# The overflow branch moved into the ninth expert pair, the meta tokens' reads put last, the 16 by 16 inversion cut into two 8 by 8 halves, and the first transfers reordered

## The chip, the core and the metric

The kernel runs on one core of a Trainium2 chip. The metric is device microseconds of one execution; the lower, the better. The core has TensorE (PE; its weight loads are listed as PEld), VectorE (DVE), ScalarE (ACT), GpSimd (POOL) and SyncE (SP, which here only issues DMAs); 16 DMA engines serve all queues.

## What is computed

Two layers over 528 tokens (16 meta tokens ahead of 512), 1024 channels. Cut to what matters here:

```python
for l in range(2):
    proj = h @ w_in[l]
    o_dn = deltanet_group(...)    # 4 heads; chunks need inv(I + L), L strictly lower
    o_sa = dsa_group(...)         # 8 heads, each query keeps its best 128 keys
    mix = concat(o_dn, o_sa) @ w_out[l]
    h = layer_norm(alpha * h + mix, ln1_g[l], ln1_b[l])
    ffn = hier_moe(h, ...)        # top group of 4, top 2 of its 8 experts, 32 experts
    h = layer_norm(alpha * h + ffn, ln2_g[l], ln2_b[l])
return h[:, 16:]                  # hid = silu(t @ w1) * (t @ w3); y = hid @ w2, gated
```

## The kernel before, in words

One program, both layers unrolled. A framework tracks which instruction reads and writes which tile and sets all waits. A planner, working with its own cost estimates, decides the order of each engine's queue; the order of the source is its priority, and `tc.issue_after(x)` asks that instructions of x's engine stand behind x. Each engine then runs its queue strictly in order. Large tiles (128 x 2112, fp32) come from one pool of 19 `unit`s: two hold the residual `hu`, the expert weights take most of the others.

**Start.** `begin` (L229) issues on SP six transfers: router weights `gw`, `lcol`, and four small ones (`ng`, and `alog`, `dtb`, `br` broadcast to all partitions by `bcast`, L153). Behind them come the first projection's weights `wr` (`weights`, L216: a load, for this block a scaling on POOL, L240, a rounding on ACT, L221, a remainder on POOL, L226), tiles 3 and 4 of x, the constants, the rotary tables.

**Attention part.** The list ORDER names projections, index scores, key selections, and for each pair of heads H, P (prepare), I (invert), R, E. `invert` (L647) gathers the 66 diagonal 16 by 16 blocks of I + L onto 66 partitions by a DMA round trip (`scr`), and DVE substitutes forward, row by row: 15 steps of one product (L668, up to 15 by 15 per partition) and one sum (L670). A second round trip (`scx`, L673, L675) puts the inverses back; PE then joins blocks of 16 to 32, 64 and 128 (tiles `y`, `d`), interleaved with projections. There are two inversions in each layer.

**After attention.** `w_out`, the first layer norm's statistics, routing (L1149 to L1237, a chain of some 40 short DVE instructions) and, beside it, the normalisation of the five row tiles: tiles 2 and 4 on POOL (L1111), the others on ACT (L1113); each is stored to `hs`, from which the experts' rows are gathered.

**Experts.** 32 experts in 16 pairs, 64 slots each. A pair needs six 1 MB weight loads (`load_part`, L311, tile `we`, one unit each), a gather of its rows (POOL, L1242), their transposes (`xtq`, L1372; `xT`, L1377 and L1379), 32 matmuls (`h`), the activation, 16 matmuls (`yp`), and a scatter of the gated rows into the table `ytab` (POOL, L1491); pairs 14 and 15 stay in SBUF (`yw`). Before the first pair 16 loads have been issued. In pair 2 a unit `lnu` is taken for the first norm's gain and bias; in pair 4 PE spreads them over the partitions (`lnp`), in pairs 5 and 6 DVE applies them to the residual (`rescale`, L1419). In layer 0, pair 8 also issues `begin` for the next layer.

**Overflow.** An expert with more than 64 tokens has its rest worked off under `tc.If(n_extra > 0)` (L1505), behind the last pair: a loop that loads that expert again, adds into the residual, and uses four units. With these inputs `n_extra` is 0 and the branch is jumped over in both layers; every engine still runs it.

**The layer's end.** In pair 15 `fetch_rows` (L1429; meta tile L1434) reads the two contributions of each row back from `ytab` in the order of the norm list, in layer 0 tiles 1, 2, meta, 3, 4, in layer 1 tiles 1 to 4; then the second norm's rows (`row_quarters`, L168; `lnw`, L1468). DVE adds them to the residual (`merge_rows`, L1440). Behind the branch PE adds pairs 14 and 15 (`cmb`), DVE adds that to the residual (L1407), and the second norm follows (L1618 to L1646); then the next layer's first projection, or the output.

Of the kernel before, what the change touches and what calls it, by code (L numbers as in the profile page):

```python
# [16 lines left out]
F32 = mybir.dt.float32  # L17
# [47 lines left out]
def trunk(ctx, tc, a, out, dbg=None, depth=DEPTH, stop=None):  # L65
# [163 lines left out]
    def begin(l):  # L229
# [4 lines left out]
        nc.sync.dma_start(lcol, a["ln1_c"][l])  # L234
        ng = spool.tile([P, 1], F32, name="ng")
        nc.sync.dma_start(ng, a["ng"][l])
        return gw, lcol, ng, bcast(a["alog"], l, 4, "alog"), bcast(a["dtb"], l, 4, "dtb"), bcast(a["b_r"], l, 36, "br")
# [36 lines left out]
    for l in range(depth):  # L274
# [372 lines left out]
        def invert(Hs, LT, full):  # L647


            Db, Xb, tm = Hs[0].spare[:, 0:256], Hs[0].spare[:, 256:512], Hs[1].spare[:, 0:256]  # L650
# [12 lines left out]
            Dv = Db.rearrange("p (j i) -> p i j", j=16)  # L663
            Xr = Xb.rearrange("p (r c) -> p r c", r=16)
            Xv = Xb.rearrange("p (r c) -> p c r", r=16)
            tv = tm.rearrange("p (r c) -> p r c", r=16)
            for i in range(1, 16):
                nc.vector.tensor_tensor(tv[:NB, :i, :i], Xv[:NB, :i, :i], Dv[:NB, i:i + 1, :i].to_broadcast([NB, i, i]),  # L668
                                        op=OP.mult)
                nc.vector.tensor_reduce(Xr[:NB, i, :i], tv[:NB, :i, :i], axis=AX.X, op=OP.add, negate=True)  # L670
            X16 = tm[:, :128].rearrange("p (q c) -> p q c", q=8)
# [641 lines left out]
        def expert_hidden(xT, ws):  # L1313

            cs = range(len(ws[0]))
            n = 64 * len(cs)
            p1 = pa("h13")
            for k in range(KT):
                for c in cs:
                    fed = _mm(nc, p1[64 * c:64 * c + 64], xT[:, k, 64 * c:64 * c + 64],  # L1320
                              ws[k // 2][c][:, k % 2 * 512:k % 2 * 512 + 512], start=(k == 0), stop=(k == KT - 1))
# [6 lines left out]
        def expert_out(hid, ws):  # L1328

            cs = range(len(ws[0]))  # L1330
            n = 64 * len(cs)
# [6 lines left out]
            for j in range(2):  # L1338
                for f in range(2):
                    for c in cs:  # L1340
                        fed = _mm(nc, p3[j][64 * c:64 * c + 64], hidT[:, f * n + 64 * c:f * n + 64 * c + 64],
                                  ws[j][c][:, 512 * f:512 * f + 512], start=(f == 0), stop=(f == 1))
            return p3, fed

        def gated(p3, gate, yh, yl, n=P):

            for j in range(2):
                p = p3[j][:n]
                done = nc.scalar.activation(yh[j][:n], p, AF.Copy, scale=gate[:n])
                nc.vector.scalar_tensor_tensor(yl[j][:n], p, gate[:n], yh[j][:n], op0=OP.mult, op1=OP.subtract)  # L1350
# [7 lines left out]
        def slots(toks, tag="r"):  # L1358

            G = tpool.tile([P, T + 3], F32R, name="G", tag=tag, bufs={"t": 5, "r": 2}[tag])  # L1360
# [3 lines left out]
        def halves(name, tag):  # L1364
            return [tpool.tile([P, T + 3], F32R, name=name, tag=tag, bufs=5)[:, 0:512] for j in range(2)]
# [44 lines left out]

        rowed, merged, late = {}, {}, []
# [10 lines left out]
        def fetch_rows():  # L1422

            for t in norder:
                o = OFF[t] - q0
                if t:
                    merged[t] = unit(f"yr{t}")
                    for i in range(2):
                        nc.sync.dma_start(merged[t][:, i * D:(i + 1) * D], ytab[i * rows + o:i * rows + o + P, :])  # L1429
                else:  # L1430
                    merged[t] = lnwq[:, 6 * D // 4:2 * D]
                    for i in range(2):
                        for q in range(4):
                            nc.sync.dma_start(merged[t][32 * q:32 * q + 16, i * D // 4:(i + 1) * D // 4],  # L1434
                                                ytab[i * rows:i * rows + 16, q * D // 4:(q + 1) * D // 4])
# [6 lines left out]
        for pair in range(16):  # L1442
            if pair == 8 and l + 1 < depth:
                with tc.issue_after(loaded[0].ins):
                    begun = begin(l + 1)
            if pair == 2:
# [11 lines left out]
            if pair == 15:  # L1458
# [4 lines left out]
                fetch_rows()  # L1463
                if 0 in tiles_q:
                    row_quarters(lnwq, 1, l)
                for i, nm in enumerate(("_g", "_b")):
                    src = a["ln2" + nm]
                    nc.sync.dma_start(lnw[:, i * D:(i + 1) * D],  # L1468
                                      bass.AP(tensor=src.tensor, offset=src.offset + l * D, ap=[[0, P], [1, D]]))
# [4 lines left out]
            hid, fed = expert_hidden(xT, ws[:4])  # L1474
            if pair == 0:
                gate_table()
            if pair == 4:
# [9 lines left out]
            p3, fed = expert_out(hid, ws[4:])  # L1487
# [14 lines left out]
        ttab = dpool.tile([1024 + P, 1], I32, name=f"ttab{l}")  # L1502
        wtab = dpool.tile([1024 + P, 1], F32, name=f"wtab{l}")
        etab = dpool.tile([16, 64], I32, name=f"etab{l}")
        with tc.If(n_extra > 0):  # L1505
            ov = unit("ov")
            area[:] = [ov[:, 0:T], 0]
            none = spool.tile([P, 9], I32, name="none", bufs=1)
            nc.vector.memset(none, 4096)
            nc.sync.dma_start(ttab[:, :].rearrange("(p c) o -> p (c o)", p=P), none)  # L1510
            zero = spool.tile([P, 9], F32, name="zero", bufs=1)
            nc.vector.memset(zero, 0.0)
            nc.sync.dma_start(wtab[:, :].rearrange("(p c) o -> p (c o)", p=P), zero)

            cum = [ov[:, (i + 1) * T:(i + 2) * T] for i in range(2)]
            nc.vector.tensor_copy(cum[0][:, :32], nb)
            ci = 0
            for s in (1, 2, 4, 8, 16):
                nc.vector.tensor_copy(cum[1 - ci][:, :s], cum[ci][:, :s])
# [230 lines left out]
```

## Time and profile before

| | us |
|---|---|
| median of 3 runs | 1441.79 (1438.68 to 1449.44) |
| the profiled execution's own time | 1439.81 |
| its span, first to last instruction | 1438.0 |
| around the span | 1.8 |

The mean granted TensorE clock of the profiled execution is 0.944 of full speed. The span falls into these stretches: layer 0's attention part to about 380, `w_out` and routing to 455, its experts to 699, its end to 732; in layer 1 the same at 1085, 1157, 1405 and 1438. A timeline row reads: start, length, engine, source line, operation, tiles written and read, how many in a row, and in brackets the idle time ahead of the first and what ended it. A letter q behind an engine marks its queue (waits, branches and DMA issues).

### The profile page before, as it was taken

The numbers are of one execution on the slowest core, as the hardware profiler recorded it, in microseconds if no ns is written. First come the engines' busy times: TensorE is split into PE (matmuls) and PEld (weight loads), VectorE is DVE, ScalarE is ACT, GpSimd is POOL, SyncE is SP. The second block draws the span as 40 slices with busy tenths as digits, with TensorE's granted clock in tenths as the row PEclk, the third lists the DMA queues.
The fourth block names the chain that finished last, engine by engine and source line by source line (L and its number), as shares of the span: only waits on it lengthen the run. The fifth ranks groups of instructions, "written<-read, shape, count | busy, mean of one in ns | idle before, by whom it ended". The sixth has DMA issues, their size and how long they took to land.

```text
span 1438.0 us, 23990 instructions
## 1 busy us (share of the span) xinstructions
PE 1262.4 (88%) x8664; PEld 896.7 (62%) x8664; DVE 794.0 (55%) x2088; ACT 542.3 (38%) x1385; POOL 596.5 (41%) x779
## 2 busy tenths in 40 slices
PE   6999999899996997888578999998999699978884
PEld 6998998787893332222268988997887443322222
DVE  4887999767336131111578889996663531311126
ACT  3574544355322222222136655352552122222222
POOL 4557497845023112111154584897332232111102
PEclk9999999899997999999899999998799899998997
DMA  4252222223716999999721531322255389999982
GB/s 168 82 194 76 68 83 86 71 90 128 282 61 257 392 409 372 410 410 397 288 96 68 198 89 58 101 83 67 75 212 228 140 329 409 409 409 410 409 334 81
DMA packets 103692, 306.55 MB, mean 213 GB/s; under 512 B 24567, under 2 KB 25671, under 8 KB 103568
## 3 DMA queue, kind: packets, MB, share of 16 engines
q1 hardware_dynamic: 88464, 274.11, 50.4%
q0 software_dynamic: 9184, 18.00, 3.4%
q10 hardware_dynamic: 5920, 12.85, 2.4%
q8 instruction: 70, 1.15, 0.3%
q14 instruction: 54, 0.44, 0.1%
HBM read 281.49 MB, written 32.19 MB: 218 GB/s over the span
## 4 chain that ended last, share of the span: by engine, by line
PE 25%; DVE 12%; issue 6%; ACT 3%; DMA 2%; POOL 2%; SPq 1%; POOLq 0%; DVEq 0%; ACTq 0%; another core or an unknown queue 0%
PE h L61 7%; PE pj L61 5%; PE yp L61 4%; DVE scores L496 2%; DVE top L495 2%; PE po L986 1%; DMA ytab<-yw,dest 1%; DVE dn L668 1%; PE lgp L61 1%; PE d L61 1%; DVE dn L521 1%; PE xtq L1372 1%; PE ptp L978 1%; PE y L61 1%; POOL wl L226 1%
## 5 line engine op out<-in xcount | busy, mean ns | idle before, releaser
L226 POOL TENSOR_TENSOR wl<-wr,wh 128x256 fp32r<-128x256 f32 (+1 forms) x296 | 251.9, 881 | 218.2 <-ACT wh L221 177.9
L61 PE MATMUL h<-we,xT 128*64 128x512 f32 x1024 | 229.3, 599 | 0.2
L61 PE MATMUL pj<-hh,wh 128*128 128x264 f32 (+2 forms) x928 | 163.2, 312 | 5.5 <-ACT raw L338 1.9
L61 PEld LDWEIGHTS h<-we,xT 128*64 128x64 f32 x1024 | 73.6, 140 | 145.2 <-issue 133.4
L61 PE MATMUL yp<-we,hidT 128*64 128x512 f32 x512 | 139.5, 684 | 26.8 <-ACT yw L1354 23.1
L61 PE MATMUL pj<-hl,wh 128*128 128x264 f32 (+2 forms) x928 | 161.0, 307 | 0.9 <-DVE rs L1623 0.9
L61 PE MATMUL pj<-hh,wl 128*128 128x264 f32 (+2 forms) x928 | 160.7, 306 | 0.2 <-POOL wl L226 0.2
L61 PEld LDWEIGHTS pj<-hh,wh 128*128 128x128 f32 (+1 forms) x928 | 133.7, 195 | 12.3 <-ACT raw L338 2.1
L1241 POOL MEMSET xe<- 128x1024 f32 x32 | 30.4, 952 | 267.3 <-PE h L61 252.4
L61 PEld LDWEIGHTS pj<-hl,wh 128*128 128x128 f32 (+1 forms) x928 | 135.1, 193 | 7.0 <-DVE rs L1623 1.1
L61 PEld LDWEIGHTS pj<-hh,wl 128*128 128x128 f32 (+1 forms) x928 | 132.0, 191 | 5.5 <-issue 0.4
L1324 DVE SCALAR_TENSOR_TENSOR hid<-hid,h 128x256 f32<-128x256 f32 x32 | 13.5, 421 | 214.1 <-ACT hid L1323 214.1
L221 ACT CAST wh<-wr 128x1024 fp32r<-128x1024 f32 (+1 forms) x82 | 85.5, 1045 | 88.0 <-PE pj L61 38.5
L1323 ACT ACTIVATE hid<-h 128x256 f32<-128x256 f32 x32 | 12.3, 383 | 229.3 <-PE h L61 217.8
L1379 ACT ACTIVATE xT<-xtq,lcol 128x128 f32<-128x128 f32 x192 | 73.4, 455 | 59.3 <-PE xtq L1372 58.7
L61 PEld LDWEIGHTS yp<-we,hidT 128*64 128x64 f32 x512 | 35.8, 149 | 95.3 <-issue 58.4
L1377 DVE TENSOR_SCALAR xT<-xtq,lcol 128x128 f32<-128x128 f32 x64 | 26.2, 410 | 119.9 <-ACT xT L1379 119.9
L521 DVE SCALAR_TENSOR_TENSOR dn<-cin,cw,dn 128x528 f32<-128x528 f32 x72 | 64.0, 898 | 10.0 <-ACT dn L519 8.9
L1491 POOL DMA_INDIRECT ytab<-yw,dest x28 | 28.2, 1005 | 88.7 <-ACT xT L1379 45.8
L496 DVE MATCH_REPLACE8 scores<-top,scores 128x144 f32<-128x144 f32 (+3 forms) x128 | 62.0, 487 | 0.1
L495 DVE MAX8 top<-scores 128x8 f32<-128x144 f32 (+3 forms) x128 | 60.5, 494 | 0.3
L1334 PE MATMUL hidT<-cst,hid 128*128 128x128 f32 x64 | 14.0, 300 | 39.7 <-DVE hid L1325 39.7
(432 smaller groups left out, 2434.9 us busy)
## 6 DMA issues: line engine op xcount, KB each, us to landing
we<-w SPq DMA_DIRECT2D x190, 1024.0 KB, 19.1
wr<-w_in SPq DMA_DIRECT2D x64, 512.0 KB, 3.3
wr<-w_out SPq DMA_DIRECT2D x16, 512.0 KB, 3.7
yr<-ytab SPq DMA_DIRECT2D x16, 512.0 KB, 10.5
ytab<-zr ACTq DMA_DIRECT2D x16, 264.0 KB, 3.3
hu<-x SPq DMA_DIRECT2D x8, 512.0 KB, 5.3
hs<-hu ACTq DMA_DIRECT2D x8, 512.0 KB, 4.8
ytab<-zr ACTq DMA_DIRECT2D x16, 256.0 KB, 3.2
```

What stands on the lines that cost most here:

```text
L61: return nc.tensor.matmul(out, lhsT=lhsT, rhs=rhs, start=start, stop=stop)
L221: nc.scalar.copy(hi[:, :KT * m], raw)
L226: eng.tensor_tensor(lo[:, c], raw[:, c], hi[:, c], op=OP.subtract)
L495: nc.vector.max(top, sc)
L496: nc.vector.match_replace(out=sc, in_to_replace=top, in_values=sc, imm_value=GONE)
L521: nc.vector.scalar_tensor_tensor(dst, cin[:, j:j + T], cw[:, ci + j:ci + j + 1], dst, op0=OP.mult, op1=OP.add)
L668: nc.vector.tensor_tensor(tv[:NB, :i, :i], Xv[:NB, :i, :i], Dv[:NB, i:i + 1, :i].to_broadcast([NB, i, i]), op=OP.mult)
L978: nc.tensor.transpose(p[:, (tk - 1) * P:tk * P], lg[:, OFF[tk]:OFF[tk] + P], ident)
L1241: nc.gpsimd.memset(xe, 0.0)
L1377: last = nc.vector.tensor_scalar(xT[:, kk, :], src, g_, b_, op0=OP.mult, op1=OP.add)
L1379: nc.scalar.activation(xT[:, kk, :], src, AF.Identity, bias=b_, scale=g_)
L1491: nc.gpsimd.indirect_dma_start(out=ytab[:, :], out_offset=bass.IndirectOffsetOnAxis(ap=dest[:, pair:pair + 1], axis=0), in_=yw[:, :], in_o ...
```

## The change

1. The overflow branch becomes a function, called at the top of pair 8 in each layer, behind the loads of pairs 8, 9 and 10. Its body loads its weights into other tiles, takes no unit, and writes its rows through `ytab`; after pair 15 there is no branch. `lnu` is taken in pair 6 in place of 2, `lnp` moves from pair 4 to 9, `rescale` from pairs 5 and 6 to 10 and 11.
2. `fetch_rows` takes one tile: tiles 1 to 4 are read first, then the second norm's rows, `row_quarters`, and the meta tile last. The four large tiles' merges stand together in pair 15; the meta tile's moves into its own `norm_stats`. The next layer's first weights are asked for behind the last of the norm's rows on SP.
3. The inversion treats both diagonal 8 by 8 blocks of each 16 by 16 block in the same instructions (7 steps) and gets the lower left block by two products of 512 elements and two sums.
4. `begin` is split: at the start, the four small transfers go behind the first weights, tiles 3 and 4 of x, and the constants.
5. All five tiles are normalised on ACT.

The diff, cut to its core:

```diff
-    begun = begin(0)
-    begun += (weights(0, 32, MISC, extra=begun[:2]),)
+    begun = begin_router(0)
+    first = weights(0, 32, MISC, extra=begun)
     fetch(h, spill, (3, 4))
     nc.sync.dma_start(cst[:, P:], a["cst"][:, P:])
+    begun += (*begin_rest(0), first)
     tables = rotary()
...
-            for i in range(1, 16):
-                nc.vector.tensor_tensor(tv[:NB, :i, :i], Xv[:NB, :i, :i], Dv[:NB, i:i + 1, :i].to_broadcast([NB, i, i]), op=OP.mult)
-                nc.vector.tensor_reduce(Xr[:NB, i, :i], tv[:NB, :i, :i], axis=AX.X, op=OP.add, negate=True)
+            for i in range(1, 8):
+                tv = tm[:NB, :2 * i * i].rearrange("p (b c r) -> p b c r", b=2, c=i)
+                nc.vector.tensor_tensor(tv, Xd[:, :, :i, :i].rearrange("p b r c -> p b c r"),
+                                        Dd[:, :, None, :i, i].to_broadcast([NB, 2, i, i]), op=OP.mult)
+                nc.vector.tensor_reduce(Xd[:, :, i, :i], tv, axis=AX.X, op=OP.add, negate=True)
+            for a_, b_, dst, neg in (...):
+                nc.vector.tensor_tensor(prod, a_[:, :, None, :].to_broadcast([NB, 8, 8, 8]),
+                                        b_[:, None, :, :].to_broadcast([NB, 8, 8, 8]), op=OP.mult)
+                nc.vector.tensor_reduce(dst, prod, axis=AX.X, op=OP.add, negate=neg)
...
-            if t in (2, 4):
-                nc.gpsimd.tensor_scalar(x, x, rs[:n, t:t + 1], nmr[:n, t:t + 1], op0=OP.mult, op1=OP.add)
-            else:
-                nc.scalar.activation(x, x, AF.Identity, bias=nmr[:n, t:t + 1], scale=rs[:n, t:t + 1])
+            nc.scalar.activation(x, x, AF.Identity, bias=nmr[:n, t:t + 1], scale=rs[:n, t:t + 1])
...
         for pair in range(16):
+            if pair == 8:
+                for ahead in range(3):
+                    load_pair(8 + ahead)
+                overflow()
             if pair == 8 and l + 1 < depth:
                 with tc.issue_after(loaded[0].ins):
-                    begun = begin(l + 1)
-            if pair == 2:
+                    begun = begin_router(l + 1) + begin_rest(l + 1)
+            if pair == 6:
                 lnu = unit("lnu")
...
-                fetch_rows()
+                for t in norder:
+                    if t:
+                        fetch_rows(t)
+                for i, nm in enumerate(("_g", "_b")):
+                    last_read = nc.sync.dma_start(lnw[:, i * D:(i + 1) * D], ...)
                 if 0 in tiles_q:
                     row_quarters(lnwq, 1, l)
-                for i, nm in enumerate(("_g", "_b")): ...
-                with tc.issue_after(fed.ins):
-                    for t in norder[:2]:
-                        merge_rows(t)
+                    fetch_rows(0)
...
-            if pair == 4:
+            if pair == 9:
                 with tc.issue_after(fed.ins):
                     for r in rowed["gb"]:
                         row_bcast(r)
-            if pair in (5, 6):
-                rescale(torder[:3] if pair == 5 else torder[3:])
+            if pair in (10, 11):
+                rescale(torder[:3] if pair == 10 else torder[3:])
             if pair == 15:
                 with tc.issue_after(fed.ins):
-                    for t in norder[2:]:
-                        merge_rows(t)
+                    for t in norder:
+                        if t:
+                            merge_rows(t)
...
-            with tc.issue_after(done.ins):
+            with tc.issue_after(done.ins), tc.issue_after(last_read.ins):
                 begun += (weights(l + 1, 32, MISC, extra=begun[:2]),)
-        with tc.If(n_extra > 0):
-            ov = unit("ov")
...
         def norm_stats(t, evac, mode):
+            if t == 0:
+                merge_rows(t)
```

## Rows read from the trace of the kernel before

**Rows 1.** Page, part 1: busy us (share of the span), instructions.

```profile
PE 1262.4 (88%) x8664; PEld 896.7 (62%) x8664; DVE 794.0 (55%) x2088; ACT 542.3 (38%) x1385; POOL 596.5 (41%) x779
```

**Rows 2.** Windows, layer 1's experts: PE, PEld, DVE, ACT, POOL; clock, DMA share, GB/s.

```profile
1170.00:1270.00 100.00, 90.33 (x407) 31.25 (x402) 24.54 (x41) 25.75 (x62) 19.85 (x20) 0.97 1.02 407
1270.00:1380.00 110.00, 89.64 (x384) 30.87 (x382) 16.27 (x34) 25.43 (x62) 16.86 (x18) 0.91 1.02 408
```

**Rows 3.** DMA issues from 1170 to 1380: count, KB each, median us to landing.

```profile
we<-w SPq DMA_DIRECT2D x75, 1024.0 KB, 20.7
ytab<-yw,dest POOLq DMA_INDIRECT x13, 8.0
```

**Rows 4.** Chain of waits, layer 1: start, us, `h` of pairs 3, 4, 5, 8, 9.

```profile
1198.61 7.04 PE h L61 x32
...
1212.22 7.04 PE h L61 x32
...
1232.08 6.89 PE h L61 x32
...
1276.85 7.58 PE h L61 x32
...
1294.19 7.44 PE h L61 x32
```

**Rows 5.** Timeline, layer 0's end.

```profile
684.04 1.76 SPq L1429 DMA_DIRECT2D yr<-ytab  x4
...
687.21 13.22 SPq L1434 DMA_DIRECT2D lnwq<-ytab  x8
...
711.95 7.16 PE L61 MATMUL cmb<-yw,G 128*128 128x512 f32 x48 [12.50 <-DVEq L1505]
...
714.03 0.69 DVE L1407 CUSTOM_DVE_ANT_0 hu<-hu,cmb 128x512 f32<-128x512 f32 x1 [2.29 <-PE cmb L61]
```

**Rows 6.** Source line L1440, both layers: ns min/median/max, first and last start.

```profile
L1440 DVE TENSOR_TENSOR hu<-hu,yr x16: 1211/1218/1695, 698.9 to 1411.6; 128x1024 f32<-128x1024 f32 x16
```

**Rows 7.** Timeline, layer 1's end.

```profile
1389.44 4.76 SPq L1429 DMA_DIRECT2D yr<-ytab  x8
...
1413.03 3.75 PE L61 MATMUL cmb<-yw,G 128*128 128x512 f32 x8 [7.83 <-DVEq L1505]
...
1415.11 0.69 DVE L1407 CUSTOM_DVE_ANT_0 hu<-hu,cmb 128x512 f32<-128x512 f32 x1 [2.29 <-PE cmb L61]
```

**Rows 8.** Waits, whole span: us in total, times, longest.

```profile
PE y L61 <- DVE scores L681: 13.7, 4, 5.3
```

**Rows 9.** Windows, behind layer 1's second inversion; columns as Rows 2.

```profile
1000.00:1010.00 10.00, 10.00 (x161) 8.89 (x156) 2.29 (x6) 3.96 (x9) 0.00 (x0) 0.50 0.07 24
```

**Rows 10.** Timeline, the start.

```profile
3.54 0.63 SPq L236 DMA_DIRECT2D ng<-ng  x1
...
5.82 0.33 SPq L216 DMA_DIRECT2D wr<-w_in  x1
...
12.52 0.67 POOL L240 TENSOR_TENSOR wr<-gw,lcol 128x288 f32<-128x288 f32 x1 [11.08 <-DMA wr<-w_in]
```

**Rows 11.** Groups by line, the substitution: busy us, mean ns of one.

```profile
L668 DVE TENSOR_TENSOR dn<-dn 66x1 f32<-66x1 f32 (+14 forms) x60 | 30.6, 509 | 2.9 <-DMA dn<-scr 1.5
...
L670 DVE TENSOR_REDUCE dn<-dn 66x1 f32<-66x1 f32 (+14 forms) x60 | 13.9, 232 | 1.4
```

**Rows 12.** Source line L579: ns min/median/max.

```profile
L579 DVE TENSOR_TENSOR dk<-ktp,Bc x8: 676/678/680, 82.3 to 960.6; 128x512 f32<-128x512 f32 x8
```

**Rows 13.** Timeline, layer 0's routing.

```profile
437.02 0.35 DVE L1151 TENSOR_TENSOR rta<-rta 128x180 f32<-128x180 f32 x1
...
438.54 1.22 DVE L1153 TENSOR_TENSOR rta<-rta,br 128x180 f32<-128x180 f32 x1
```

**Rows 14.** Source line L1505, layer 1: SP's branch and its nine waits.

```profile
L1505 SPq EVENT_SEMAPHORE  x9: 17/17/17, 1395.8 to 1405.6; - x9
...
L1505 SPq COMPARE_BRANCH  x1: 50/50/50, 1395.3 to 1395.3; - x1
```

More of the change, by code (lines that the diff above doesn't have):

```diff
@@ L227, in weights, with begin_router @@
         return hi, lo
-    def begin(l):
+    def begin_router(l):
         gw = spool.tile([P, KT, 36], F32, name="gw", bufs=1)
@@ L234, in begin, with begin_rest @@
         nc.sync.dma_start(lcol, a["ln1_c"][l])
+        return gw, lcol
+    def begin_rest(l):
         ng = spool.tile([P, 1], F32, name="ng")
         nc.sync.dma_start(ng, a["ng"][l])
-        return gw, lcol, ng, bcast(a["alog"], l, 4, "alog"), bcast(a["dtb"], l, 4, "dtb"), bcast(a["b_r"], l, 36, "br")
+        return ng, bcast(a["alog"], l, 4, "alog"), bcast(a["dtb"], l, 4, "dtb"), bcast(a["b_r"], l, 36, "br")
     def scaled_router(dst, gw, lcol):
@@ L662, in invert @@
             nc.gpsimd.memset(Xb[:, 0:256:17], 1.0)
[L663 to L666, printed above, removed]
[L667 to L671 removed]
+            Dd, Xd = (H.spare[:NB, 0:272].rearrange("p (b x) -> p b x", b=2)[:, :, 0:128].rearrange("p b (r c) -> p b r c", r=8)
+                      for H in Hs)
+            for i in range(1, 8):
[3 more added lines that the diff above has]
+                nc.vector.tensor_reduce(Xd[:, :, i, :i], tv, axis=AX.X, op=OP.add, negate=True)
+            half = Hs[0].spare[:NB, 400:464].rearrange("p (j c) -> p j c", j=8)
+            prod = tm[:NB].rearrange("p (a c k) -> p a c k", a=8, c=8)
+            Xr = Xb[:NB].rearrange("p (r c) -> p r c", r=16)
+            Lr = Db[:NB].rearrange("p (j i) -> p i j", j=16)
+            for a_, b_, dst, neg in ((Lr[:, 8:, :8], Xr[:, :8, :8].rearrange("p k c -> p c k"), half, False),
+                                     (Xr[:, 8:, 8:], half.rearrange("p k c -> p c k"), Xr[:, 8:, :8], True)):
+                nc.vector.tensor_tensor(prod, a_[:, :, None, :].to_broadcast([NB, 8, 8, 8]),
+                                        b_[:, None, :, :].to_broadcast([NB, 8, 8, 8]), op=OP.mult)
+                nc.vector.tensor_reduce(dst, prod, axis=AX.X, op=OP.add, negate=neg)
+            X16 = Hs[0].spare[:, 272:400].rearrange("p (q c) -> p q c", q=8)
             scx = dpool.tile([NB, 256], F32, name="scx", bufs=2)
@@ L1313, in expert_hidden @@
         def expert_hidden(xT, ws):
-            cs = range(len(ws[0]))
-            n = 64 * len(cs)
             p1 = pa("h13")
             for k in range(KT):
+                if k % 2 == 0:
+                    w = ws(k // 2)
+                cs = range(len(w))
+                n = 64 * len(cs)
                 for c in cs:
                     fed = _mm(nc, p1[64 * c:64 * c + 64], xT[:, k, 64 * c:64 * c + 64],
-                              ws[k // 2][c][:, k % 2 * 512:k % 2 * 512 + 512], start=(k == 0), stop=(k == KT - 1))
+                              w[c][:, k % 2 * 512:k % 2 * 512 + 512], start=(k == 0), stop=(k == KT - 1))
             hid = mpool.tile([P, 2 * P], F32, name="hid", tag="vnew")[:n]
@@ L1328, in expert_out @@
         def expert_out(hid, ws):
-            cs = range(len(ws[0]))
-            n = 64 * len(cs)
+            n = hid.shape[0]
+            cs = range(n // 64)
             p2 = pb("hidT")
@@ L1356, in gated_rows, with slots @@
             return done
-        def slots(toks, tag="r"):
-            G = tpool.tile([P, T + 3], F32R, name="G", tag=tag, bufs={"t": 5, "r": 2}[tag])
+        def slots(toks):
+            G = tpool.tile([P, T + 3], F32R, name="G", tag="r", bufs=2)
             nc.gpsimd.tensor_scalar(G[:, 0:T - q0], tid[:, 0:T - q0], toks, None, op0=OP.is_equal)
             return G
-        def halves(name, tag):
-            return [tpool.tile([P, T + 3], F32R, name=name, tag=tag, bufs=5)[:, 0:512] for j in range(2)]
         def transpose_rows(xe, xT):
@@ L1420, in rescale, with fetch_rows @@
                 nc.vector.scalar_tensor_tensor(x, b_, ALPHA, x, op0=OP.mult, op1=OP.add)
[L1422 to L1435, printed above, removed]
+        def fetch_rows(t):
+            o = OFF[t] - q0
+            if t:
+                merged[t] = unit(f"yr{t}")
+                for i in range(2):
+                    nc.sync.dma_start(merged[t][:, i * D:(i + 1) * D], ytab[i * rows + o:i * rows + o + P, :])
+            else:
+                merged[t] = lnwq[:, 6 * D // 4:2 * D]
+                for i in range(2):
+                    for q in range(4):
+                        nc.sync.dma_start(merged[t][32 * q:32 * q + 16, i * D // 4:(i + 1) * D // 4],
+                                          ytab[i * rows:i * rows + 16, q * D // 4:(q + 1) * D // 4])
         def merge_rows(t):
```

188 lines of the change are left out of this document (96 added, 92 removed).

## The prediction, made before the changed kernel ran

> **What bounds the kernel now.** I read the page's busy times first, then windows by stage, then the chain of waits, the waits by pair of engines, and timelines of each layer's end and of the start. TensorE is busy 1262.4 us of 1438.0 [rows 1], so 176 us of idle time are the most that better order alone could give, and most of that lies where transfers set the pace.
>
> In the experts the DMA engines do. From 1170 to 1380 their share reads 1.02 at 407 and 408 GB/s in both windows, while PE has 90% [rows 2]; 75 loads went out in these 210 us, 2.8 us for each with all that shares the engines [rows 3]. The chain shows both paces: 13.6 us from pair 3's `h` to pair 4's, when weights asked for earlier lie ready (PE's own pace), 17.3 from pair 8's to pair 9's, when six loads have to arrive (6 x 2.8 = 16.8) [rows 4]. Pair 4 takes 19.9: it holds `lnp`, which adds 6.2.
>
> At the layer ends DVE and its branch do. In layer 0, `yr` of the first two tiles is issued at 684.04, SP then issues the meta tile's eight reads for 13.22 us, so tiles 3 and 4 follow only at about 700.5; PE, free at 711.95 - 12.50 = 699.45, waits for the branch in DVE's queue [rows 5], which stands behind the merges (1.22 us each) [rows 6]. In layer 1 PE is free at 1413.03 - 7.83 = 1405.2 and waits for the same; the merges' last begins at 1411.6 [rows 6, 7].
>
> In the attention part PE is almost never idle, but at each of the four inversions it waits for the chain through DVE, 13.7 us in all, the longest 5.3 [rows 8]. Behind such a wait it can run on at half clock: 0.50 over 1000 to 1010, with PE busy all 10 us [rows 9].
>
> **The change part by part.** *Start, -2 us.* Four small transfers stand ahead of the first weights, from 3.54 to 5.82, and POOL waits 11.08 us for these until 12.52 [rows 10]. Moved behind, they give up to 2.3. The large transfers for x now share the engines with nothing new ahead of `wr`; the small ones are needed by router and gates much later. Range 0 (x's tiles set the start as well) to 3 gained; I take 2.
>
> *Inversions, -7.* Now 15 products (mean 509 ns) and 15 sums (232 ns) take 11.1 us of DVE each time [rows 11]. Afterwards 7 small products and 7 sums remain; with two blocks at once they have up to 98 elements per partition, inside the sizes of today's, so below the mean: I take 330 and 190 ns, 3.6 us. The two products of 512 elements are priced by a product of that size, 0.68 each [rows 12], the sums over the same 512 as much: 2.7 together. So 6.4 in place of 11.1: 4.7 less in each of the four chains. The waits that can shrink are 2.9, 4.1, 1.4 and 5.3 us (the total and the longest are in [rows 8]): at most 2.9 + 4.1 + 1.4 + 4.7 = 13.1. Against taking all: DVE is nearly full there, and what a shorter chain frees is taken by other due work first, whose order the planner makes afresh. For more: if PE never waits, the stretch at half clock may go too, worth up to 5 us in ten [rows 9]; four at 3 us make 12. Bounds: a loss of 1 and a gain of 25; I take half the waits, 7.
>
> *Normalising on ACT, -1.* In routing DVE's operation of 180 elements took 0.35 us alone and 1.22 while POOL normalised a tile [rows 13]; two such meetings a layer, some 1.5 us of a chain that all the experts wait for. But ACT has two tiles more to do, and the gather waits for the last tile's store as well. I take 0.5 a layer; 0 to 3 in all.
>
> *The branch in pair 8, both layers.* What it costs there: each engine drains its own work, then jumps. SP's nine waits stretch from 1395.8 to 1405.6 today, behind a branch at 1395.3 [rows 14], since its reads were still on the way; in pair 8 up to eight loads are. So no load is issued until the last of them has landed. No row shows a full stream stopped and begun again. From below it costs 0, if new loads overlap the drain of the rest; from above 8.0, one landing of the scatter in the same stretch [rows 3]. I take 2.7, near one load's 2.8, because the stream has only to refill. Against that stands the unit that `lnu` no longer holds until pair 6: one load goes earlier, 2.8. The two cancel.
>
> PE has to wait until pair 7's rows are evacuated, jump, and wait for the next transposes. From 0.5 (branch alone, [rows 14]) to 12.5 (the worst wait at today's branch, [rows 5]); I take the middle, 6.5. Of this pair 8 already loses 17.3 - 13.6 = 3.7 to the loads [rows 4], which hides that much.
>
> Layer 1's experts then have two limits. PE: pair 3 begins at 1198.61, so pair 0 at 1198.61 - 3 x 13.6 = 1157.8; 16 x 13.6 + 6.2 (`lnp`) + 6.5 = 230.3 brings it to 1388. DMA: SP came to the rows' reads at 1389.44 [rows 7], which stays, 2.7 - 2.8 being nothing. With half a pair behind the last load (7.6, the longest `h` [rows 4]) PE ends at 1397 rather than 1405.2. Today it lags because `lnp` sits in pair 4, at PE's own pace; in pair 9 the 6.2 us fall where PE waits for loads.
>
> *The ends.* Layer 1: the rows' reads, 4.2 MB at 408 GB/s [rows 2], take 10.3 us, to 1399.5. Two merges of 1.22 behind the last make 1402. Without the branch there, `cmb` begins when PE and its banks are free, and L1407 follows `cmb` by 2.1 [rows 7]; with the merges between, I put it at 1405 against 1415.11: **-10** (5 to 13). Layer 0: tiles 1 to 4 are issued together from 684, land by about 697, are merged by 702. PE is free at about 699.45 as today, and L1407 comes at 705 against 714.03 [rows 5]. What is late next is the meta tile: its 13.22 us of issues now end near 707, and it stands third in this layer's norm list, so I return 1: **-8** (3 to 13). `rescale` in pairs 10 and 11 and the meta tile's merge are DVE work beside PE, and DVE is 16 to 25% busy there [rows 2].
>
> Sum: 2 + 7 + 1 + 8 + 10 = 28. The profiled execution took 1439.8; less 28 that is 1411.8. The median of the runs lies 2.0 above it, so the forecast is **1414**.
>
> [...] The trace shows SP half a microsecond from its branch to what follows [rows 14], at a time when the weights' stream had ended. [...]
>
> **The rivals.** *B: the pace does not recover.* Pairs 8 to 12 stay at 17.3, the drain at the branch costs the 8.0, and the ends give only what `cmb`'s wait gave in part. For it: the DMA share is 1.02 [rows 2], so lost DMA time is never made up. Against it: today's PE ends 16 us behind 1389, which the loads don't ask for. Price: layer 1's experts lose 8.0 - 2.7 = 5.3 of their 10, layer 0 the same of 8, the inversions give 2: 28 - 10.6 - 5 = 12, so about 1430.
>
> *C: the wait takes the branch's place, and the kernel is slower.* In pair 8 PE is made to wait, through the data behind the branch, for POOL's drain: a scatter (8.0 us, [rows 3]) must land before POOL jumps, then the gather and the transposes begin, which nothing ran ahead of. One such stall is 8 + 6.5 = 14.5 us; PE then runs at half clock for some 14 us, losing another 7 [rows 9]. [...] It decides from 14 us net of a stall per layer, when the 28 are gone. For it: one register and one branch on all engines, with gathers on POOL's queue. Against it: gathers are issued pairs ahead, and the 12.5 at today's branch was DVE's merges, not POOL's scatter.
>
> *D: more than forecast.* The inversions give the waits and the clock as well: 25 rather than 7, so 1396 or less. Against it: PE would have to find other work at all four places.
>
> *E: the edits miss the path.* The planner puts merges and `cmb` as late as before, and other chains end the inversions: ends 5 in all, no more from the inversions: 1442 - 8 = 1434.
>
> **How the numbers follow.** The forecast (1397 to 1426) has 0.56, D 0.10, B 0.16, E 0.09, C 0.09. The range: 1392, the forecast less 22 (18 of D and 4 from the ends), to 1437, behind B and E; outside it lie C and a small part of D. About 1% (14.4 us) is what a measurement of this kernel can tell from no change: faster by over 1% means under 1427.4, which holds for the forecast and D, 0.66, and a third of B, 0.05: 0.71. Within 1%: the rest of B, E and a little of C: 0.22. Slower, above 1456: 0.07.
>
> **What would show it.** Right: no wait of DVE L1505 ahead of `cmb`; L1407 about 8 and 10 us sooner, measured from each layer's routing; SP's reads of tiles 3 and 4 in one row with 1 and 2; waits `PE y <- DVE scores` nearer 7 than 13.7; DVE's busy time down by some 19 us; the first `pj` 2 us sooner; around the branch a dent in the DMA share of under 5 us. Wrong: PE idle for over 14 us in pair 8, pairs behind it at 17.3 up to the last with PE ending at 1405 or later (by the old start), or a half clock right behind the branch; in the attention part, waits moved to other tiles with the same sum.

## The result, and the profile after

The changed kernel takes 1451.04 us (median of 14 runs, 1447.72 to 1460.58), the kernel before 1441.68 in its 14: a ratio of 1.0073, with a 95% interval of 1.0053 to 1.0092. It is slower by about 9 us; the prediction said faster by 28, and its range ended at 1437.

Where the time went, stage by stage, from the starts and ends of PE's instructions in the two timelines (us):

| from | to | before | after |
|---|---|---|---|
| start | layer 0's first `h` | 455.8 | 460.6 |
| there | layer 0's last `yp` | 243.7 | 258.8 |
| there | layer 1's first projection | 32.5 | 31.5 |
| there | layer 1's first `h` | 425.1 | 420.3 |
| there | layer 1's last `yp` | 248.2 | 247.0 |
| there | end of the span | 32.8 | 29.8 |

Not each of these differences is the change's. Up to layer 0's first `h` nine of the kernels below run the same instructions in the same order on PE, DVE, ACT and POOL as the changed kernel, and reach it at 454.2 to 463.9. Stages of the attention part are therefore compared over several profiles. The experts' stages vary too: `f3_inversion_alone`, below, has PE's instructions there in the order of the kernel before and the same 23.1 us of waits for ACT, and takes 241.7 and 241.4 us instead of 243.7 and 248.2, at a granted clock of 0.98 and 0.96 instead of 0.96 and 0.94. What is compared there is therefore PE's idle time: in layer 0's experts it grew from 35.0 to 47.3 us, and that is the finding. The ends differ by at most 0.9 us between the changed kernel and six of the kernels below, so it is a finding too that they gave 1.0 and 3.0 in place of 8 and 10.

Medians of different sets of runs also differ without a cause in the kernel: `e5_merges_early` turned out to have the changed kernel's instructions in the changed kernel's order throughout, and read 4.0 us more.

The page of the changed kernel, part 1; it answers to [rows 1]:

```profile
PE 1267.1 (88%) x8664; PEld 900.0 (62%) x8664; DVE 780.5 (54%) x2040; ACT 547.2 (38%) x1389; POOL 598.3 (41%) x775
```

Its waits, in total, times, longest; the second row answers to [rows 8]:

```profile
PE h L61 <- ACT xT L1390: 29.4, 3, 10.3
PE y L61 <- DVE scores L696: 9.2, 3, 6.8
PE yp L61 <- ACT yw L1368: 4.9, 2, 2.4
```

The same view of the kernel before has a row that the prediction did not read:

```profile
PE yp L61 <- ACT yw L1354: 23.1, 12, 2.4
```

No row of either list in the experts says that PE waited for a load, though the DMA engines' share read 1.02 [rows 2]. PE waited for ACT, which gated the previous pair's rows (`yw`) late, twelve times, 1.9 us on average. After the change most of these waits are gone (4.9 instead of 23.1), but three for `xT` stand there, about 10 us each: one in pair 8 of each layer, one in pair 9 of layer 0.

Pair 8 of layer 1, timeline (an engine's q marks its queue; in brackets idle time and what ended it):

```profile
1283.94 0.97 POOL L1599 DMA_INDIRECT ytab<-yw,dest  x1 [8.75 <-ACT yw L1368]
...
1288.34 0.69 ACT L1368 ACTIVATE yw<-yp,gtab 128x512 f32<-128x512 f32 x1 [4.91 <-issue]
...
1289.12 1.09 PE L1383 MATMUL xtq<-cst,xe 128*128 128x128 f32 x8 [0.88 <-ACTq L1428]
1292.10 0.97 POOL L1599 DMA_INDIRECT ytab<-yw,dest  x1 [7.18 <-DMA ytab<-yw,dest]
1299.49 2.21 ACT L1390 ACTIVATE xT<-xtq,lcol 128x128 f32<-128x128 f32 x6 [10.46 <-DMA xe<-hs,gix]
...
1300.00 2.83 PE L61 MATMUL h<-we,xT 128*64 128x512 f32 x6 [9.78 <-ACT xT L1390]
```

PE, ACT and DVE are past the branch (L1428) at 1289. POOL still has two scatters one behind the other, pair 6's at 1283.94 and pair 7's at 1292.10, which lands at 1299.10; POOL's drain ends there, and the semaphore of POOL's transfers on which ACT's `xT` waits is set behind it, at 1299.40. The bracket names a gather; but the gathers ahead of the branch had landed by 1257.5 and 1271.1, so it is not their transfer that was late. This is rival C's mechanism at rival C's place.

Pair 9 of layer 0, timeline:

```profile
607.34 0.46 SPq L232 DMA_DIRECT2D gw<-w_r  x1
...
609.01 0.46 SPq L153 DMA_DIRECT2D alog<-alog  x1
...
614.73 0.20 ACT L423 ACTIVATE eal<-alog 128x4 f32<-128x4 f32 x1 [13.02 <-DMA alog<-alog]
614.84 1.14 ACT L1390 ACTIVATE xT<-xtq,lcol 128x128 f32<-128x128 f32 x3
...
615.33 1.12 PE L61 MATMUL h<-we,xT 128*64 128x512 f32 x2 [9.34 <-ACT xT L1390]
```

SP reached the branch at 588.3 and left its drain at 606.3, when the eight loads under way had landed. Only then did it issue `begin`'s small transfers. ACT has work on `alog` ahead of pair 9's `xT` and stood 13.0 us at it, and PE behind ACT.

Each stall costs more than itself. In pair 8 of layer 0 the granted clock is 0.50 over 585 to 590, while PE stands, still 0.57 over 590 to 595, and 1.00 over 595 to 605; `h` behind the stall takes 9.02 us instead of 7.04:

```profile
590.38 9.02 PE L61 MATMUL h<-we,xT 128*64 128x512 f32 x32 [10.29 <-ACT xT L1390]
```

It takes 9.20 in pair 8 of layer 1 and 8.50 in pair 9 of layer 0.

### The profile page after: what moved, and what is told of

Read it like the earlier page. It is cut to its first block, busy times and chain, and to the rows that moved or that the text cites. A ratio compares the mean times of both kernels' runs of the same rounds, so it can differ in the third digit from the quotient of the medians.

```text
span 1447.9 us, 23972 instructions
## 1 busy us (share of the span) xinstructions
PE 1267.1 (88%) x8664; PEld 900.0 (62%) x8664; DVE 780.5 (54%) x2040; ACT 547.2 (38%) x1389; POOL 598.3 (41%) x775
## 5 line engine op out<-in xcount | busy, mean ns | idle before, releaser
L61 PE MATMUL h<-we,xT 128*64 128x512 f32 x1024 | 232.7, 607 | 29.6 <-ACT xT L1390 29.4
L61 PE MATMUL yp<-we,hidT 128*64 128x512 f32 x512 | 133.3, 665 | 9.9 <-ACT yw L1368 4.9
L61 PEld LDWEIGHTS pj<-hh,wl 128*128 128x128 f32 (+1 forms) x928 | 135.6, 197 | 5.7 <-POOL wl L226 0.7
L501 DVE MATCH_REPLACE8 scores<-top,scores 128x400 f32<-128x400 f32 (+3 forms) x128 | 62.1, 489 | 0.1
L500 DVE MAX8 top<-scores 128x8 f32<-128x400 f32 (+3 forms) x128 | 60.7, 496 | 0.2
L172 POOL TENSOR_TENSOR rs<-rs,mhalf 128x1 f32<-128x1 f32 (+1 forms) x11 | 12.6, 1144 | 106.2 <-DVE rs L1647 74.1
```

Source lines behind the costliest of these rows:

```text
L61: return nc.tensor.matmul(out, lhsT=lhsT, rhs=rhs, start=start, stop=stop)
L172: return nc.gpsimd.tensor_tensor(dst, src, expo[:n, :w], op=OP.pow)
L500: nc.vector.max(top, sc)
L501: nc.vector.match_replace(out=sc, in_to_replace=top, in_values=sc, imm_value=GONE)
```

## The experiments

Times are medians; each ratio is to the kernel before in the same set of runs.

**Is it the branch?** `e1_no_branch` drops the call from the changed kernel.

```diff
                 for ahead in range(3):
                     load_pair(8 + ahead)
-                overflow()
```

> The changed kernel without the overflow branch in either layer (the rows over 64 per expert are left out; with these inputs there are none). Theory A, the branch in pair 8 is the loss: in the changed kernel's profile pairs 7 to 9 took 27.3, 25.0 and 21.2 us in layer 0 and 26.6, 15.7 and 18.2 in layer 1; without it those of PE's own pace (13.6, 19.8 with lnp) come back as far as the loads allow, so layer 0's experts (first h to last yp) shrink from 258.8 to about 235 and layer 1's from 247.0 to about 235: 1449.7 - 36 = 1414, 1408 to 1422. Rival B, the loads set the pace: the pairs behind go back to 17.3, little is won, 1440 or more.

Measured: 1448.9, 1.0032 (0.9994 to 1.0069). Theory A fell: without any branch the changed kernel is hardly better. Layer 0's experts still take 258.5, layer 1's 249.8. PE's idle time in layer 0's fell by 8.3 us, but its busy time rose by 8.0 for the same instructions, so this profile is a poor witness there; the median is the better one. ACT waits 13.1 us for `alog` here too, since the small transfers stand behind the loads of pairs 8 to 10 on SP.

`e3_begin_first` keeps the branch and moves `begin` ahead of those loads:

```diff
+            if pair == 8 and l + 1 < depth:
+                with tc.issue_after(loaded[0].ins):
+                    begun = begin_router(l + 1) + begin_rest(l + 1)
             if pair == 8:
                 for ahead in range(3):
                     load_pair(8 + ahead)
                 overflow()
-            if pair == 8 and l + 1 < depth:
-                with tc.issue_after(loaded[0].ins):
-                    begun = begin_router(l + 1) + begin_rest(l + 1)
```

> The changed kernel with the next layer's small transfers issued ahead of the branch's loads and the branch in pair 8 rather than behind. Theory A: in layer 0 ACT stood 13.0 us at alog, which SP issued only behind its drain, and PE 9.3 us at the xT behind it; that goes, and 6 to 11 us of 1449.7 with it: 1439 to 1444. Rival B, pair 9 would wait for its loads anyway, as SP issued none from 586 to 606: 0 to 3, 1447 to 1450.

Measured: 1439.6, 0.9964 (0.9935 to 0.9993), 11.5 us under the changed kernel; layer 0's experts fall from 258.8 to 251.0, layer 1's take 245.1. The second stall of layer 0 was no part of the branch as such, but of what stood behind it on SP.

`e6_no_branch_begin_first` is both edits together.

> The changed kernel with the next layer's small transfers first and without the branch (the rows over 64 are left out). Against the one with small transfers first (1439.6) this is the price of the branch in pair 8 alone. Theory A': PE's own order, not the loads, sets the pace, and the branch costs about 10 us of PE in each layer, part of it made up by pairs that no longer wait for ACT's yw: 1428 to 1434. Rival B: the same as with the branch, 1437 to 1442, since what the branch costs is made up behind it.

Measured: 1443.8, 0.9997 (0.9967 to 1.0027); experts 251.1 and 246.5, as with the branch. This is 2 us above rival B's range and far from theory A's, and the waits say why; those of `e6_no_branch_begin_first`:

```profile
PE yp L61 <- ACT yw L1368: 20.4, 10, 2.4
```

and of `e3_begin_first`:

```profile
PE h L61 <- ACT xT L1390: 21.4, 2, 11.7
...
PE yp L61 <- ACT yw L1368: 4.9, 2, 2.4
```

With the branch PE has two waits of 10 to 12 us for `xT` and two for `yw`; without it, ten for `yw`. The totals are near each other (26 and 20), and so are the times. The planner orders the queues anew around the branch, and behind it ACT's `yw` no longer comes late.

`e4_scatter_behind` takes a scatter out of POOL's drain: pair 7's rows stay in a unit until the branch is past.

```diff
                 overflow()
+                scatter(7, held_yw)
```

> The changed kernel with pair 7's scatter issued behind the branch (its rows in a unit meanwhile), so that POOL drains one scatter less. Theory A: PE's 9.8 and 10.3 us at pair 8's xT are POOL's drain of that scatter (landed 1299.1, xT at 1299.5); they fall to 2 to 3 in each layer; 8 to 16 off 1449.7, so 1434 to 1442. Rival D, ACT waits in its own branch or for SP's drain: the wait stays at 10, 1448 to 1452.

Measured: 1443.0, 1.0009 (0.9984 to 1.0035), 8 us less than the changed kernel. PE's waits for `xT` went from 29.4 us to one of 2.5, those for `yw` rose from 4.9 to 11.6:

```profile
PE yp L61 <- ACT yw L1368: 11.6, 5, 2.4
...
PE h L61 <- ACT xT L1390: 2.5, 1, 2.5
```

Pair 8's waits, 10.3 and 9.8 us, fell to 2.5 and none, so it was POOL's drain there, as theory A said (its range ended 1 us lower). Pair 9's 9.3 us in layer 0 went for another reason: the planner's new order has ACT's work on `alog` only in pair 10, and ACT no longer waits for it:

```profile
628.02 0.21 ACT L423 ACTIVATE eal<-alog 128x4 f32<-128x4 f32 x1
```

`e7_both` adds this to `e3_begin_first`:

> The changed kernel with the small transfers first and pair 7's scatter behind the branch. If the two losses are separate they add: 1451.0 - 11.5 - 8.0 = 1431.5, 1428 to 1436. If both are the same slack (the loads' end), 1438 to 1443.

Measured: 1439.4, 0.9966 (0.9937 to 0.9995): they don't add. `e4_scatter_behind` had no stall at `alog` left that `begin` in front could remove: its experts take 247.4 and 245.2 us, those here 247.6 and 245.2. And of each `xT` wait removed, part came back as waits for `yw` (10.5 us here).

**Do loads hide `lnp`?** `f4_lnp_back` is `e3_begin_first` with `lnu`, `lnp` and `rescale` where they were.

```diff
-            if pair == 9:
+            if pair == 4:
                 with tc.issue_after(fed.ins):
                     for r in rowed["gb"]:
                         row_bcast(r)
```

> The changed kernel with the small transfers first, and lnu, lnp and rescale back in pairs 2, 4, 5 and 6. Theory G, PE is never held by loads, so lnp's 6.2 us cost the same anywhere, and pair 6's wait for yw (18.1 instead of 13.6) only moves a pair further: 1437 to 1442 against 1439.6. The forecast's theory, lnp is hidden behind loads in pair 9 and not in pair 4: 5 to 6 more, 1445.

Measured: 1439.4, 0.9980 (0.9958 to 1.0001), against 1439.6 for `e3_begin_first`. This is theory G's range: nothing shows that loads hid `lnp` in pair 9.

**The ends.** In the changed kernel `cmb` no longer waits for a branch, and yet the first projection comes 31.5 us behind the last `yp`. Layer 0's end there, SP's and DVE's timelines; these answer to [rows 5]:

```profile
701.42 3.79 SPq L1532 DMA_DIRECT2D yr<-ytab  x8
...
714.16 6.75 SPq L1537 DMA_DIRECT2D lnwq<-ytab  x8
...
718.43 0.75 DVE L1364 SCALAR_TENSOR_TENSOR yw<-yp,gtab,yw 128x512 fp32r<-128x512 f32 x1 [3.71 <-DMA lnwq<-ytab]
719.09 1.22 DVE L1543 TENSOR_TENSOR hu<-hu,yr 128x1024 f32<-128x1024 f32 x1
...
750.86 1.74 PE L61 MATMUL pj<-hh,wh 128*116 128x264 f32 x8 [1.97 <-DVE hl L186]
```

And windows (PE, PEld, DVE, ACT, POOL; clock, DMA share, GB/s):

```profile
700.00:710.00 10.00, 9.92 (x49) 4.07 (x49) 2.32 (x4) 3.95 (x9) 0.00 (x0) 1.00 0.83 317
710.00:720.00 10.00, 8.09 (x37) 2.73 (x34) 2.41 (x4) 2.02 (x4) 0.00 (x0) 1.00 0.73 273
720.00:730.00 10.00, 6.59 (x44) 3.16 (x42) 10.00 (x17) 1.36 (x3) 0.00 (x0) 0.83 0.31 108
730.00:740.00 10.00, 4.00 (x23) 2.31 (x21) 9.89 (x18) 5.30 (x11) 9.52 (x8) 0.88 0.35 128
```

DVE is idle for three quarters of 700 to 720 and full for 20 us from 720, because its merges stand behind pair 15's gated rows. (The bracket at 718.43 names a transfer; but DVE's `yw` reads ACT's, which ended at 718.39.) The kernel before had merged while PE stood at the branch. What the branch no longer costs, the merges now cost.

`e5_merges_early` asks for the merges ahead of pair 15's `h` in the source.

> The changed kernel with the four tiles' merges asked for ahead of pair 15's h rather than behind it. Theory E, the ends give nothing because the merges (eight of 1.22 us) now run behind PE's last yp: in the changed kernel DVE is idle up to 718 and merges from 719.1 to 732.8, so the first projection stands 31.5 us behind the last yp as before (32.5). If they run beside pair 15, 5 to 9 us go at each layer's end: 1451 - 14 = 1437, 1433 to 1443. Rival F, what is late are the rows' transfers or the meta tile: 0 to 4 in all, 1447 to 1451.

Measured: 1455.1 (4 runs), 1.0081 (1.0051 to 1.0111), but this tells nothing of either theory: the order stayed the changed kernel's on PE, DVE, ACT, POOL and SP, the first merge at 720.7 still behind the gated rows. `f5_after_forced` holds the order itself:

```diff
+            if pair == 15:
+                for t in big[:2]:
+                    mine = merge_rows(t)
+                behind.enter_context(tc.issue_after(mine.ins))
+            with behind:
                 hid, fed = expert_hidden(xT, lambda j: ws[j])
...
+            with behind:
                 done = gated(p3, gate, yh, yl)
```

> The changed kernel with the merges held by order: two tiles ahead of pair 15's activation on DVE, two ahead of its gated rows, the meta tile's behind the second tile's statistics (asking for them earlier had left DVE's order as it was, first merge still behind the gated rows). Theory E: DVE's 13 idle us between 700 and 719 take the eight merges (9.8 us), the first projection comes 5 to 9 us sooner behind layer 0's last yp (31.5 becomes 23 to 27), layer 1's end 3 to 8: 1451 - 12 = 1439, 1434 to 1444. Rival F: the first projection waits for the meta tile's and tile 4's transfers or for ACT, 29 to 31.5 stays: 1447 to 1452.

Measured: 1443.4, 1.0016 (0.9985 to 1.0046), 7.6 less than the changed kernel; the first projection comes 22.8 us behind the last `yp` instead of 31.5, the end 25.4 instead of 29.8. Its DVE in layer 0:

```profile
701.36 4.87 DVE L1543 TENSOR_TENSOR hu<-hu,yr 128x1024 f32<-128x1024 f32 x4
...
710.57 3.61 DVE L1543 TENSOR_TENSOR hu<-hu,yr 128x1024 f32<-128x1024 f32 x3
...
719.27 0.69 DVE L1418 CUSTOM_DVE_ANT_0 hu<-hu,cmb 128x512 f32<-128x512 f32 x1 [2.15 <-PE cmb L61]
```

Theory E holds here: DVE's order, not the branch or the transfers, bounds the end. Part of the gain is given back: the experts' stages take 0.4 and 2.7 us more, with merges ahead of pair 15's activation.

**The parts without the branch, and the inversion.** `e2_branch_last` is the kernel before with every edit but the branch's.

> The kernel before with every other edit (first transfers, reads' order and merges, halves of the inversion, normalising on ACT), but with the old branch behind pair 15 and lnu, lnp and rescale where they were. Theory A: what is lost lies in the branch alone; the rest is worth the 3 us that layer 1's attention and the ends show, so 1432 to 1441. Rival C, the inversion is the loser (layer 0's first h came 4.8 us later): 1442 to 1450. By the forecast's own terms (2 + 7 + 1 and about 5 of the ends) it would be 1427.

Measured: 1447.2, 1.0034 (1.0006 to 1.0062): in rival C's range, and 20 us off the forecast's own terms. Not the inversion alone does it: layer 0's experts take 242.6, layer 1's 241.4, but layer 0's end grew from 32.5 to 40.6 us. The branch is not what grew: measured from the last `yp`, the merges begin as before (0.3 us ahead of it, 0.5 in the kernel before), and PE waits 10.1 us for the branch instead of 12.5. What is late stands behind it. ACT has a rounding of the next layer's weights ahead of the second norm, these weights now stand behind the norm's rows on SP, and ACT waits for them, DVE and PE for ACT:

```profile
725.31 1.04 ACT L221 CAST wh<-wr 128x1024 fp32r<-128x1024 f32 x1 [3.62 <-DMA wr<-w_in]
...
728.34 2.08 PE L61 MATMUL cmb<-hu,cst 128*128 128x512 f32 x2 [5.28 <-DVE sums L1419]
```

`e8_old_inversion` is the changed kernel with the substitution row by row.

> The changed kernel with the old inversion, row by row. DVE's busy time in four inversions was 44.5 us before and 33.0 in the changed kernel, PE's waits for them 13.7 and 9.2. Forecast's theory: the halves are worth 4 to 10, so this takes 1455 to 1461. Rival C: they are worth nothing or lose, since other work fills DVE and the round trips stay: 1446 to 1453.

Measured: 1444.7, 1.0022 (0.9995 to 1.0049): 6.3 less with the *old* inversion, below both ranges. `f3_inversion_alone` puts the new one alone into the kernel before.

> The kernel before with the inversion in halves and nothing else. By the forecast's term: 1441.7 - 7 = 1435. By what undoing it in the changed kernel gave (1451.0 to 1444.7): 1446 to 1449, since y is put ahead of 16 projection products and PE waits for it longer at the second inversion (6.9 us there instead of 4.2), the big products take 1.1 to 2.1 us beside POOL and the round trips stay. No effect: 1440 to 1444.

Measured: 1443.6, 1.0011 (0.9983 to 1.0039): nothing. With these two apart, the question went to further bases, below. What the new chain costs on DVE, from the changed kernel's source lines (ns min/median/max):

```profile
L683 DVE TENSOR_TENSOR scores<-dn x8: 1061/1197/2078, 111.2 to 1003.8; 66x512 f32<-66x512 f32 x8
...
L685 DVE TENSOR_REDUCE dn<-scores x8: 667/676/682, 112.9 to 1005.8; 66x64 f32<-66x512 f32 x8
```

The sums cost what was forecast, the big products 1.1 to 2.1 us instead of 0.68 (1.37 on average), the 28 small products 409 ns on average instead of 330. One chain's end in layer 0, DVE and POOL beside each other:

```profile
260.09 1.33 POOL L354 TENSOR_TENSOR raw<-raw,sw 128x528 f32<-128x528 f32 x1
260.27 2.08 DVE L683 TENSOR_TENSOR scores<-dn 66x512 f32<-66x512 f32 x1
...
271.52 2.75 POOL L226 TENSOR_TENSOR wl<-wr,wh 128x256 fp32r<-128x256 f32 x4
272.90 2.91 DVE L696 TENSOR_SCALAR scores<-dn,cst 128x128 f32<-128x128 f32 x2 [5.08 <-DMA dn<-scx]
...
275.86 3.06 PE L61 MATMUL y<-scores,lx 32*32 32x32 f32 x64 [6.85 <-DVE scores L696]
```

The substitution ended 2.6 us sooner than before (265.8, 268.5), but the two selections (L696) behind the round trip took 2.91 us beside POOL instead of 0.48, and `y` began at 275.9 where it had begun at 276.1. One of the two took 2.73; the others that ran beside POOL in these two traces took 0.28 to 0.78, so the size of this one stays unexplained. All eight big products (L683) and their sums (L685) ran beside POOL, at 1.06 to 2.08 us and 0.67 to 0.68 us, so no row shows what either takes without it. PE stood there 6.85 us and not 4.15: `y` was queued ahead of 16 projection products (`pj`) that stood before it in the old order.

**What beats both.** `f1_begin_old_inv` is `e3_begin_first` with the old inversion.

> The changed kernel with the small transfers first and the old inversion. If the two losses are separate, 1451.0 - 11.5 - 6.3 = 1433, 1430 to 1437; if the gain of the old inversion was scatter of the clock, 1437 to 1442.

Measured: 1435.9, 0.9948 (0.9925 to 0.9972). `f2_forced_merges` adds the merges' order of `f5_after_forced`.

> The same with the merges held by order as well. Theory E: 8 to 12 below it, about 1423, which would be faster than both kernels; rival F: within 3 of it.

Measured: 1433.2, 0.9940 (0.9916 to 0.9963): faster than both kernels by 8 and 18 us, though 2.7 below the kernel beside it, not the 8 to 12 of theory E but rival F's "within 3"; on this base the merges' order is not shown to gain. Its ends are as short as forecast (25.1 and 25.4), but its experts' stages read 255.2 and 250.4 where `f1_begin_old_inv` reads 248.1 and 246.9. PE is idle 3.6 and 2.9 us longer in them, which fits merges that stand ahead of pair 15's activation; the rest goes with a lower clock in layer 0 (0.93 and 0.94).

`g1_all_mended` adds pair 7's scatter behind the branch, `g2_mended_halves` the new inversion on top of that.

> The version with small transfers first, the old inversion and the merges held (1433.2), and pair 7's scatter behind the branch as well. If PE's 10 us at pair 8's xT are still a loss there, 4 to 8 less: 1425 to 1430. If pairs behind the branch again wait for ACT's yw instead, as they did when the same was added to the small transfers first (1439.6 to 1439.4), no change: 1431 to 1436.

> The same with the inversion in halves: a third base for it, after one where undoing it gave 6.3 us and one where adding it alone gave nothing. Halves lose in themselves: 3 to 7 more than the kernel beside it. Worth nothing: within 2. By the forecast: 7 less.

Measured: 1433.9, 0.9945 (0.9923 to 0.9966), and 1441.0, 0.9985 (0.9964 to 1.0006). The scatter gives nothing more; the halves lose 7.1 us on this base.

## Why the prediction was wrong

**Where the difference lies.** The change was to shorten the span by 28 us, and by the two profiles it lengthened it by 9.9. Of these 38 us, 22 lie in layer 0's experts and end (8 less forecast, 14.1 more found), 6 in layer 1's (10 less forecast, 4.2 found), 10 in the start, inversions and routing (10 less forecast, nothing found).

**The bound.** The step that failed first was the reading of [rows 4]: "17.3 from pair 8's to pair 9's, when six loads have to arrive (6 x 2.8 = 16.8)". The two numbers lie near each other by chance. The 17.3 are PE's own 13.6, 1.8 for ACT's `yw`, and the rest `h` and `yp` at a lower granted clock (`h` 7.44 to 7.58 us instead of 7.04 in the same rows, clock 0.91 [rows 2]):

```profile
1291.10 3.09 PE L61 MATMUL yp<-we,hidT 128*64 128x512 f32 x8 [1.82 <-ACT yw L1354]
```

Counted back from the layer's last load, pair 9's six had landed by 1287.4, 6.6 us ahead of its `h`. The other limit, SP at the rows' reads at 1389.44, was misread in the same way: layer 1's last load was issued at 1371.0, and SP then stood until pair 13's scatter landed at 1389.4. Layer 1's loads in the kernel before, from 1080 on:

```profile
L311 SPq DMA_DIRECT2D we<-w x84: 367/2277/6814, 1079.8 to 1371.0; - x84
```

In the changed kernel the stream fell to 142 and 229 GB/s over 595 to 615, a dent of 10 us where under 5 was forecast, and no wait of PE ends with a load. So "in pair 9 the 6.2 us fall where PE waits for loads" was wrong (`f4_lnp_back`), and so were the 3.7 us that were to hide part of the stall. The loads are not far behind as a limit, though: in layer 0 of the kernel before, their lead over PE shrinks from pair to pair, to 3 us and less in pair 15 (the first of its six landed at 681.4, its `h` began at 684.45), and in `e2_branch_last` and `f3_inversion_alone`, whose PE is 1 to 2 us faster in layer 0's experts, it does wait for them (total, times, longest; in this order):

```profile
PE h L61 <- DMA we<-w: 3.0, 5, 0.8
...
PE h L61 <- DMA we<-w: 1.9, 3, 0.6
```

**The branch.** This is the step that cost most. Forecast 6.5 us of PE, 3.7 of it hidden; found 9.8 and 10.3 in pair 8 and 9.3 in pair 9 of layer 0, and 1.5 to 2.2 more for each in `h` at the low clock. The middle between 0.5 and 12.5 had no row behind it. The jump itself took 0.5 us on SP (588.28 to 588.77) with the loads' stream at 408 GB/s, no more than in [rows 14]. Rival C named the mechanism, POOL's scatter ahead of POOL's drain, but not its second half, `begin` behind SP's drain. Its 14.5 us for a stall and 7 more at half clock were too much as well: the stalls took 9.3 to 10.3 us, the half clock cost about 2 us a stall, the planner's new order took 18 us of `yw` waits out, and with `begin` in front the branch costs nothing that can be measured (1439.6 and 1443.8).

**The inversions.** Forecast -7; found over kernels whose sources differ in them alone: +6.3, +7.1 and +3.7 (1439.6 against 1435.9), and +1.2 on the kernel before. The last two are no more than what two sets of runs of the same order differed by. The term "0.68 each" was mis-sized (1.06 to 2.08), and so was the small products' 330 ns (409), so four chains gave 11.5 us of DVE and not 19. That the chain's end brings `y` forward failed at the second inversion. In five profiles with the old inversion and twelve with the new, the first `y` of layer 0 stands 83.0 to 84.5 us behind the first gating product in the old and 78.4 to 81.4 in the new; the second 227.1 to 232.0 and 224.4 to 230.2; in layer 1 the second 228.3 to 230.4 and 229.6 to 236.2. From the gating product to the last `po` it is on average 327.1 and 313.3 with the old, 329.5 and 316.0 with the new: PE's waits for `y` fell from some 13 to 7 to 11, but the two stages grew by 5 together. Why they grow is not shown: beyond the order, the mean clock is lower in layer 0 (0.952 instead of 0.964), but the same in layer 1 (0.954).

**The ends.** Forecast -18, found -4. Of "Tiles 1 to 4 are issued together from 684, land by about 697, are merged by 702" the last step failed. The reads wait for pair 13's scatter and moved with PE: they were issued in one row, 18.0 us ahead of layer 0's last `yp` (15.4 in the kernel before), and had landed 4.0 us ahead of it, where the forecast has 2.5. But the merges stood behind pair 15's gated rows. The branch's wait went as forecast. I asked what is late next and looked at transfers only, not at DVE's queue.

**Start and routing.** The first projection came 2.8 us sooner (11.9), as forecast, and the first gating product at 46.9 instead of 46.3: given back by 47 us. In layer 0 routing's `rank` came 1.2 us sooner behind the last `po`, the first `h` 1.1 us later behind it: PE waited for the gather there, as feared. In layer 1 `rank` came 1.6 us sooner and the first `h` another 0.6. So routing gave about 2 us, within the 0 to 3 that were forecast.

Rival E, that edits miss the path, was right for the inversions and the ends (5 forecast, 4 found), but not for the loss in the experts; B's pace argument was wrong for the reason above; D found nothing. By the forecast's own tests, the half clock behind the branch came, and PE was not idle for over 14 us in one pair, but 19.6 in two.

## What to carry to other kernels

The DMA engines' share read 1.02 here, and no row of PE's waits in the experts of the two kernels ends with a load: read what ended the idle time of the engine on the path before dividing bytes by pace. In the changed kernel the branch joined the engines: a scatter that POOL had to drain there cost PE 9.8 and 10.3 us, eight loads on SP with `alog` queued behind them 9.3. So price a branch by what each queue still has to drain there and by what is queued behind it, and issue small transfers ahead of it (11.5 us less in `e3_begin_first`). Work that ran in the shadow of a wait (here the merges) must be given a new place by order when the wait goes, and a source line moved forward does not move it where a planner decides.

## What was not expected of the hardware

In the changed kernel an engine past the branch was still held by another's drain at it: ACT was through at 1289.1 and stood until POOL's scatter had landed at 1299.10. A DVE selection of 128 elements, 0.27 us at its shortest, once took 2.73 beside POOL, others beside POOL at most 0.78. And the same instructions in the same order came to layer 0's first `h` anywhere from 454.2 to 463.9, and 31 runs of the kernel before spread from 1435.4 to 1451.3 us, the longer at a lower mean granted clock (0.947 and 0.931 at the two ends), so a stage's difference of 5 us in one profile is no evidence there.
